# Attention with negated scores: the position bias and the row extreme in one VectorE instruction

## The chip, the cores and the metric

The kernel runs on one core of a Trainium2 chip. A core has a matrix engine (TensorE, PE in the profile, with its weight loads as PEld), VectorE (DVE), ScalarE (ACT), GpSimd (POOL) and SyncE (SP), which issues the transfers (DMA). The metric is device microseconds of one execution, as the median of several runs.

## The reference

One layer of a hybrid decoder: 2048 tokens of width 1024 are normalized, projected into three branches (attention, a short gated convolution, RWKV-7 time mixing), gated, projected back, added to the input and normalized again. The change is in the attention: four heads, each with two softmax maps of 64-wide queries and keys, whose difference is applied to V. A bias that depends on the distance of query and key is added to the scores, and keys after the query are masked.

```python
logits = jnp.einsum('bqhmd,bkhmd->bhmqk', qb, kf) + bias[None, :, None]
logits = jnp.where(dist >= 0, logits, NEG_INF)
p = jax.nn.softmax(logits, axis=-1)
a = p[:, :, 0] - lam * p[:, :, 1]
return jnp.einsum('bhqk,bkhd->bqhd', a, vf)
```

## The kernel before

Products are made in float32 split into a high and a low part (three products for each full one). The tokens come in two halves of 1024. The stages follow each other: the input projection of what RWKV needs, RWKV of the first half, attention of the first half (541 to 865 us in the profile), RWKV of the second half, attention of the second half (1217 to 1805 us), the rest of the output projection. While a stage runs, products of the input projection (`inproj`, L343) and later of the output projection (`out_tile`, L1194) are put between its own on TensorE, as filler. TensorE's order is written out by hand (the generators yield how much filler they want after each step; `run` and `pull` deal it out). The order on the other engines and on the DMA queue is chosen by a scheduler that simulates the program.

In `attention`, `scores` goes through row tiles of 128 queries of one head. The keys up to the row tile's own are cut into groups of at most 512 columns, and for each group and each of the two maps there is one score block: two products into a PSUM tile `S` (L937, L938), the bias added in place where the block meets it (L942), the negated row maximum into one column of `nm` (L943), and the exponential on ScalarE with `nm` as its bias, which also sums the row into `l` (L946). There are 96 blocks in the first half and 224 in the second.

The bias differs from a constant only for the last 128 distances. The constant falls out of the softmax, so a table `bt` of 128 x 384 for each head, made in `att_setup`, holds the rest and the mask. For row tile i it reaches from column (i - 1) x 128 to the tile's end: 256 columns, or the part of them that lies in the block.

`combine` brings the groups of a row tile to one maximum (L957 to L965) and mixes the two maps (L986). `values` transposes the mixed probabilities on TensorE (L1021) into `aT`, splits them into a high part `aTh` on ScalarE (L1027) and a low part `aTl` on VectorE (L1028), and multiplies both by V (L1012 to L1014). `load_k`, `load_q` and `load_v` fetch keys, queries and values through the DMA queue and split them on GpSimd. The queries get their factor of 0.125 when they leave the input projection (`att_steps`, `in_copy`, L368).

Of the kernel before, what the change touches and what calls it, by code (L numbers as in the profile page):

```python
# [13 lines left out]
AF = mybir.ActivationFunctionType  # L14
ALU = mybir.AluOpType
# [15 lines left out]
GW = 32 // NG  # L31
# [114 lines left out]
def trunk(ctx, tc, a, o, phases="RTO"):  # L146
# [65 lines left out]
    # row blocks of the gated mix, transposed: heads by 256 tokens, conv and rwkv by 512  # L212
# [12 lines left out]
    # ------------------------------------------------------------------ normalized input  # L225
    def stats(c):
        """1/rms of the tokens of a chunk of the second half, one column per 128 tokens."""
# [38 lines left out]
    def stats0(c, xs, pool, raw):  # L266
        """1/rms of the tokens, broadcast; with raw, the products with the unscaled input come first."""
# [40 lines left out]
    # ------------------------------------------------------------------ input projection  # L308
# [97 lines left out]
    def both(*steps):  # L406
        """The products of the steps, for the first chunk of all of them before the second."""
        for c in range(2):
            for f, args in steps:
                yield from f(*args, (c,))  # L410
            yield ("chunk", c)
# [9 lines left out]
    def att_steps(half, h):  # L421
        return [(in_copy, (half, T_K + h, f"k{h}", 1.0)), (in_v, (half, h)),
                (in_copy, (half, T_Q + h, f"q{h}", 0.125)), (in_silu, (half, T_ZA + h, f"za{h}"))]
# [30 lines left out]
    # ------------------------------------------------------------------ rwkv  # L454
    def rwkv(half, pool):
# [176 lines left out]
        def inverse(s):  # L632
            U, Z = s["U"], s["Z"]
            # inverses of the 32x32 diagonal blocks by forward substitution, GW columns of one block per partition;
            # the odd rows are first freed of the even rows before them, so that two rows go at a time
# [24 lines left out]
        def late(s):  # L660
# [30 lines left out]
            # [W | U0]  # L691
# [15 lines left out]
            # transition matrices and the read-out of the incoming state  # L707
# [38 lines left out]
            # group norm, bonus, gate  # L746
# [29 lines left out]
        def chain(n):  # L776
            """The way of a unit up to the inverse; the scores may not start before the unit two back has been read."""
# [36 lines left out]
    # ------------------------------------------------------------------ attention  # L814
    def att_setup(pool):
# [15 lines left out]
        for h in range(4):  # L831
# [3 lines left out]
            nc.gpsimd.memset(bz[:, 256:], NEG)  # L835
            cpy(bz[:, 0:256], bp[:, 0:256])
# [7 lines left out]
    def attention(half, nlam, bt, pool, after=None):  # L844
        """One softmax row tile (128 queries) after the other; the matrix products with V of the pairs of tiles
        that are finished lie between the score blocks of the next ones."""
# [532 lines left out]
```

## Time and profile before

| | |
|---|---|
| median of 3 runs | 1854.19 us (1853.9 to 1865.09) |
| span of the profiled execution | 1855.8 us |
| TensorE busy | 1723.0 us, 93% |
| VectorE busy | 1228.7 us, 66% |
| ScalarE busy | 737.5 us, 40% |
| GpSimd busy | 817.9 us, 44% |

Busy times are those of the engines' own instructions in one execution. A stage is read by its window: how long each engine was busy between two times, and at which share of full speed TensorE's clock was granted. A wait names the engine, tile and line that waited, what released it, the total, how often, and the longest. The chain of work that ended last is followed back from the last instruction, at each step to what released it.

### The profile page before, as it was taken

Reading aid. Unit: us, or ns where it says so; the run is one execution under the profiler, and the core shown is the slowest. Engines: PE = TensorE matmul, PEld = TensorE weight load, DVE = VectorE, ACT = ScalarE, POOL = GpSimd, SP = SyncE. Lnnn points to the kernel's source line nnn. Section 1 sums busy time; section 2 is a strip of 40 time slices with the busy share of each in tenths; the row PEclk is TensorE's granted clock in tenths of the full one; section 3 lists DMA queues with packets and bytes.
Section 4 is the critical chain, followed back from the end, with each engine's and each line's share of the span. In section 5 each row is a group of like instructions: output and inputs, shape, how many; then the busy total and the mean of one; then the engine's idle time right before and its main releaser. Section 6 shows DMA issues by size and latency. Waiting matters only on the chain.

```text
span 1855.8 us, 27286 instructions
## 1 busy us (share of the span) xinstructions
PE 1723.0 (93%) x9416; PEld 1288.3 (69%) x9416; DVE 1228.7 (66%) x2653; ACT 737.5 (40%) x1797; POOL 817.9 (44%) x786
## 2 busy tenths in 40 slices
PE   5899799999999889999799999999999989999998
PEld 4687576777776666777666767766666666767686
DVE  7534866656527888756766576357788888777742
ACT  5331111221126555532122221145565656666642
POOL 6443332333286776334222233473485473453233
PEclk8899898998999999999799998999999989999999
DMA  5342121222156442124222222351142243232223
GB/s 181 114 146 93 47 63 59 86 76 67 61 181 196 148 140 82 64 68 148 63 82 68 86 76 62 100 154 60 63 147 64 74 150 101 71 95 70 81 78 116
DMA packets 136586, 180.13 MB, mean 97 GB/s; under 512 B 34912, under 2 KB 83072, under 8 KB 136448
## 3 DMA queue, kind: packets, MB, share of 16 engines
q1 hardware_dynamic: 136448, 178.39, 30.8%
q8 instruction: 74, 1.21, 0.3%
q14 instruction: 64, 0.52, 0.1%
HBM read 132.18 MB, written 46.14 MB: 96 GB/s over the span
## 4 chain that ended last, share of the span: by engine, by line
PE 62%; DVE 25%; DMA 4%; issue 3%; SPq 2%; ACT 2%; POOL 1%; DVEq 0%; POOLq 0%; ACTq 0%
PE pj L343 27%; PE ops L1194 9%; PE S L938 6%; DVE tmpx L646 5%; PE aT L1021 3%; PE S L937 3%; DVE Xs L649 3%; PE G L572 2%; PE av L1012 2%; DVE P L986 2%; SPq L594 2%; PE av L1014 2%; PE av L1013 2%; DVE x L242 1%; DVE nm L943 1%
## 5 line engine op out<-in xcount | busy, mean ns | idle before, releaser
L343 PE MATMUL pj<-hh,wh 128*128 128x512 f32 x1008 | 424.4, 421 | 4.2 <-DVE raw L394 3.4
L343 PE MATMUL pj<-hl,wh 128*128 128x512 f32 x1008 | 423.8, 420 | 0.0
L343 PE MATMUL pj<-hh,wl 128*128 128x512 f32 x1008 | 423.2, 420 | 0.0
L946 ACT ACTIVATE P<-S,nm 128x512 f32<-128x512 f32 (+3 forms) x320 | 199.3, 623 | 162.9 <-DVE nm L943 143.6
L943 DVE TENSOR_REDUCE nm<-S 128x1 f32<-128x512 f32 (+3 forms) x320 | 192.5, 606 | 77.4 <-PE S L938 74.1
L329 POOL TENSOR_TENSOR wl<-wr,wh 128x1024 fp32r<-128x1024 f32 x85 | 209.6, 2465 | 46.8 <-ACT wh L324 41.2
L343 PEld LDWEIGHTS pj<-hh,wh 128*128 128x128 f32 x1008 | 195.9, 194 | 49.1 <-issue 7.6
L343 PEld LDWEIGHTS pj<-hl,wh 128*128 128x128 f32 x1008 | 195.7, 194 | 45.2 <-issue 9.7
L343 PEld LDWEIGHTS pj<-hh,wl 128*128 128x128 f32 x1008 | 195.4, 194 | 45.0 <-issue 7.9
L938 PE MATMUL S<-K,QL 64*128 64x512 f32 (+2 forms) x320 | 150.1, 469 | 0.0
L326 POOL TENSOR_SCALAR wh<-wr 128x1024 fp32r<-128x1024 f32 x70 | 76.5, 1093 | 162.5 <-PE pj L343 152.6
L986 DVE SCALAR_TENSOR_TENSOR P<-P,sc 128x512 f32<-128x512 f32 (+3 forms) x160 | 141.5, 910 | 4.5 <-ACT P L970 2.9
L646 DVE TENSOR_TENSOR tmpx<-U,Xs 128x16 f32<-128x16 f32 (+15 forms) x256 | 128.6, 502 | 6.6 <-POOL U L640 1.2
L938 PEld LDWEIGHTS S<-K,QL 64*128 64x128 f32 x320 | 58.8, 184 | 101.6 <-issue 99.4
L937 PE MATMUL S<-K,QH 128*128 128x512 f32 (+2 forms) x320 | 120.8, 378 | 8.0 <-ACT P L946 8.0
L1028 DVE TENSOR_TENSOR aTl<-aT,aTh 128x512 fp32r<-128x512 f32 x144 | 98.4, 686 | 35.2 <-ACT aTh L1027 34.4
L1027 ACT CAST aTh<-aT 128x512 fp32r<-128x512 f32 x144 | 83.7, 585 | 87.9 <-PE aT L1021 87.1
L942 DVE TENSOR_TENSOR S<-S,bt 128x256 f32<-128x256 f32 (+1 forms) x152 | 57.4, 379 | 90.6 <-PE S L938 86.6
L1021 PE MATMUL aT<-con,P 128*128 128x128 f32 x576 | 93.9, 289 | 22.4 <-DVE aTl L1028 17.4
L1194 PE MATMUL ops<-woh,wl 128*128 128x512 f32 x256 | 103.9, 406 | 0.0
L1194 PE MATMUL ops<-woh,wh 128*128 128x512 f32 x256 | 103.5, 404 | 0.0
L1194 PE MATMUL ops<-wol,wh 128*128 128x512 f32 x256 | 103.5, 404 | 0.0
(336 smaller groups left out, 3354.2 us busy)
## 6 DMA issues: line engine op xcount, KB each, us to landing
wr<-in_wt_dram SPq DMA_DIRECT2D x85, 512.0 KB, 3.7
rawk<-pk SPq DMA_DIRECT2D x96, 128.0 KB, 2.8
U<-ud SPq DMA_DIRECT2D x128, 64.0 KB, 2.2
rawq<-pq SPq DMA_DIRECT2D x128, 64.0 KB, 2.3
wr<-mx SPq DMA_DIRECT2D x128, 64.0 KB, 1.9
oxt<-in_x_dram SPq DMA_DIRECT2D x32, 256.0 KB, 3.2
out_dram<-oxt SPq DMA_DIRECT2D x32, 256.0 KB, 2.1
prw<-s SPq DMA_DIRECT2D x28, 256.0 KB, 2.1
```

The lines of the kernel that those rows point to most:

```text
L329: nc.gpsimd.tensor_tensor(wl[:, ks], wr[:, ks], wh[:, ks].bitcast(F32), ALU.subtract)
L343: mm(ps, lhs[:, k], rhs[c][k], start=(n == 0), stop=(n == 3 * NK - 1))
L646: tt(tmp[:, :, :, 0:m], U[:, 0:m, i:i + 2].rearrange("p j r -> p r j").unsqueeze(2).broadcast_to([P, 2, GW, m]), Xs[:, 0:m].rearrange("p j ...
L937: mm(s[:, 0:sw], QH[:, m, off:off + P], K[:, m, 0:sw], start=True, stop=False)
L938: mm(s[:, 0:sw], QL[ms, off:off + P], K[ms, m, 0:sw], start=False, stop=True)
L943: nc.vector.tensor_reduce(nm[:, m, g:g + 1], s[:, 0:gw], AX.X, ALU.max, negate=True)
L946: act(p[:, 0:gw], s[:, 0:gw], AF.Exp, bias=nm[:, m, g:g + 1], accum_out=l[:, m, g:g + 1])
L986: stt(p1, p1, sc[:, 1, g:g + 1], p0, ALU.mult, ALU.add)
L1021: nc.tensor.transpose(t[:, d * 256 + qi * P:d * 256 + qi * P + P], x["A"][g][:, ko:ko + P], ident)
L1027: cpy(th, t)
L1028: tt(tl, t, th.bitcast(F32), ALU.subtract)
L1194: mm(ps, l[:, k], Ws[n][r][k], start=(c == 0), stop=(c == 3 * NK - 1))
```

## The change

The queries' factor and the table get the other sign, so that the scores in PSUM are negated, and the smallest score of a row is what `nm` needs. In a block that meets the bias, the columns before the bias are reduced to their minimum first (where there are any), and then one instruction adds the table to the remaining columns, writes them back, and folds their minimum with the first one (or with a large number). The exponential multiplies by -1. In a block without bias only the kind of extreme changes (a minimum, not a negated maximum). The rest of the diff removes comments.

```diff
     def att_steps(half, h):
         return [(in_copy, (half, T_K + h, f"k{h}", 1.0)), (in_v, (half, h)),
-                (in_copy, (half, T_Q + h, f"q{h}", 0.125)), (in_silu, (half, T_ZA + h, f"za{h}"))]
+                (in_copy, (half, T_Q + h, f"q{h}", -0.125)), (in_silu, (half, T_ZA + h, f"za{h}"))]
...
             bz = pool.tile([P, 512], F32, name="bz", bufs=2)
-            nc.gpsimd.memset(bz[:, 256:], NEG)
-            cpy(bz[:, 0:256], bp[:, 0:256])
+            nc.gpsimd.memset(bz[:, 256:], -NEG)
+            act(bz[:, 0:256], bp[:, 0:256], AF.Copy, scale=-1.0)
...
                     lo, hi = max(b0, g0), g0 + gw
+                    low = nm[:, m, g:g + 1]
+                    free = min(lo, hi) - g0
+                    if free > 0:
+                        nc.vector.tensor_reduce(low, s[:, 0:free], AX.X, ALU.min)
                     if hi > lo:
                         bo = lo - (i - 1) * P
-                        tt(s[:, lo - g0:gw], s[:, lo - g0:gw], bt[h][:, bo:bo + hi - lo], ALU.add)
-                    nc.vector.tensor_reduce(nm[:, m, g:g + 1], s[:, 0:gw], AX.X, ALU.max, negate=True)
+                        nc.vector.tensor_tensor_reduce(s[:, free:gw], s[:, free:gw], bt[h][:, bo:bo + hi - lo], 1.0,
+                                                       low if free > 0 else -NEG, ALU.add, ALU.min, low)
                     p = pool.tile([P, CK], F32, name="P", bufs=pb)
                     live[0] += 1
-                    act(p[:, 0:gw], s[:, 0:gw], AF.Exp, bias=nm[:, m, g:g + 1], accum_out=l[:, m, g:g + 1])
+                    act(p[:, 0:gw], s[:, 0:gw], AF.Exp, bias=low, scale=-1.0, accum_out=l[:, m, g:g + 1])
```

Lines after this place are five higher in the changed kernel (L986 is L991, L1028 is L1033, L1063 is L1068), those just before it one or none.

The first place is on VectorE, at the start of the first attention stage. A row is an instruction: its line, its kind, what it writes and reads, and the size. Before, a block is an add (L942) and a reduction (L943):

```order
L942 TENSOR_TENSOR S<-S,bt_701 128x128
L943 TENSOR_REDUCE nm<-S 128x1
L967 RECIPROCAL sc<-l 128x2
L1028 TENSOR_TENSOR aTl<-aT,aTh 128x512
L974 TENSOR_SCALAR sc<-sc,nlam 128x1
L942 TENSOR_TENSOR S<-S,bt_701 128x128
L986 SCALAR_TENSOR_TENSOR P<-P,sc 128x384
L943 TENSOR_REDUCE nm<-S 128x1
```

The same place in the changed kernel:

```order
L944 TENSOR_REDUCE nm<-S 128x1
L947 ISA S,nm<-S,bt_701,nm 128x128
L947 ISA nm 128x1
L972 RECIPROCAL sc<-l 128x2
L1033 TENSOR_TENSOR aTl<-aT,aTh 128x512
L979 TENSOR_SCALAR sc<-sc,nlam 128x1
L944 TENSOR_REDUCE nm<-S 128x1
L991 SCALAR_TENSOR_TENSOR P<-P,sc 128x384
L947 ISA S,nm<-S,bt_701,nm 128x128
L947 ISA nm 128x1
```

A block with free columns is now a reduction of these (L944), the fused instruction (L947, here "ISA", which reads `nm` too) and a second one of one column that writes the result to `nm`. A block without free columns is the last two alone. In all, 152 adds and 320 reductions before are 256 reductions, 152 fused instructions and 152 of one column after.

The second place is on VectorE, later in the first attention stage. The numbers are those of the buffers; `S_6121` before is `S_6105` after, the block of the same products, and `aTl_6134` is `aTl_6118`. Before:

```order
L1061 SCALAR_TENSOR_TENSOR ob_5947<-ob_5947,der_76,obc_6104 128x256
L986 SCALAR_TENSOR_TENSOR P_5735<-P_5735,sc_6098,P_5721 128x128
L986 SCALAR_TENSOR_TENSOR P_5703<-P_5703,sc_6098,P_5678 128x512
L942 TENSOR_TENSOR S_6121<-S_6121,bt1_710 128x256
L1028 TENSOR_TENSOR aTl_6134<-aT_6128,aTh_6133 128x512
L943 TENSOR_REDUCE nm_6062<-S_6121 128x1
```

After:

```order
L1066 SCALAR_TENSOR_TENSOR ob_5931<-ob_5931,der_76,obc_6088 128x256
L944 TENSOR_REDUCE nm_6046<-S_6105 128x1
L991 SCALAR_TENSOR_TENSOR P_5691<-P_5691,sc_6082,P_5666 128x512
L947 ISA S_6105,nm_6046<-S_6105,bt1_710,nm_6046 128x256
L947 ISA nm_6046 128x1
L1033 TENSOR_TENSOR aTl_6118<-aT_6112,aTh_6117 128x512
L991 SCALAR_TENSOR_TENSOR P_5721<-P_5721,sc_6082,P_5708 128x128
```

`aTl` stood ahead of the block's reduction and now stands behind the whole block. Of the 144 instructions of this kind, 20 are moved behind one or more further blocks in this way, and one ahead of one; of the 160 of L986, 24 are behind one more and 16 behind one fewer.

The third place is on the DMA queue, in the first attention stage: loads of keys (`rawk`), queries (`rawq`), gates (`zs`) and weights (`wr`), and stores of what the input projection made (L354) and of the attention's result (`mx`). Before:

```order
L1063 DMA mx_1_93<-ob 128x256
L998 DMA zs<-pza_0_4566 128x256
L856 DMA rawk<-pk_0_5373 64x512 x4
L354 DMA pv_0_5601<-t_5599 128x512
L884 DMA rawq<-pq_1_4444 64x256 x4
L320 DMA wr<-in_wt_dram 128x1024
```

After:

```order
L1003 DMA zs<-pza_0_4566 128x256
L320 DMA wr<-in_wt_dram 128x1024
L856 DMA rawk<-pk_0_5365 64x512 x3
L884 DMA rawq<-pq_1_4444 64x256 x2
L354 DMA pv_0_5589<-t_5587 128x512
L884 DMA rawq<-pq_1_4444 64x256 x2
L856 DMA rawk<-pk_0_5365 64x512
L320 DMA wr<-in_wt_dram 128x1024
```

The fourth load of the keys' tile is now behind loads of queries and a store.

## Rows read from the trace of the kernel before

**Rows 1.** The page: span, and busy time of two engines.
```profile
span 1855.8 us, 27286 instructions
PE 1723.0 (93%) x9416; PEld 1288.3 (69%) x9416; DVE 1228.7 (66%) x2653; ACT 737.5 (40%) x1797; POOL 817.9 (44%) x786
```

**Rows 2.** Windows: both attention stages, then a stretch of the first.
```profile
core 0: us, PE busy (x) PEld busy (x) DVE busy (x) ACT busy (x) POOL busy (x), PEclk, DMA share, GB/s
541.00:865.00 324.00, 304.30 (x1466) 223.97 (x1465) 233.26 (x508) 167.14 (x448) 191.85 (x196) 0.98 0.39 123
1217.00:1805.00 588.00, 567.96 (x2669) 402.07 (x2668) 454.73 (x856) 351.74 (x849) 285.26 (x253) 0.98 0.29 91
...
590.00:700.00 110.00, 96.28 (x455) 69.07 (x454) 90.35 (x189) 60.21 (x157) 84.00 (x81) 0.95 0.50 155
```

**Rows 3.** TensorE's waits, 541 to 865 us: total us, times, longest.
```profile
PE aT L1021 <- DVE aTl L1028: 10.0, 6, 3.4
PE av L1014 <- DVE aTl L1028: 4.9, 2, 4.2
```

**Rows 4.** TensorE's waits, 1217 to 1805 us.
```profile
PE aT L1021 <- DVE aTl L1028: 7.4, 6, 4.4
PE S L937 <- ACT P L946: 7.0, 6, 2.9
...
PE aT L1021 <- DVE P L986: 2.1, 1, 2.1
```

**Rows 5.** The chain by line: 541 to 865, 1217 to 1805, 590 to 700 us.
```profile
by line: PE pj L343 41.0%; PE S L938 8.5%; PE aT L1021 4.3%; PE S L937 4.2%; DVE P L986 4.1%; DVE xk L242 3.3%; PE av L1012 3.1%; DMA xk<-in_xT_dram 3.0%; PE av L1014 3.0%; PE av L1013 2.4%; DVE nm L943 2.4%; DVE aTl L1028 2.3%; issue 2.1%;
...
by line: PE ops L1194 21.0%; PE pj L343 15.9%; PE S L938 12.8%; PE aT L1021 8.5%; PE S L937 7.0%; PE av L1012 4.9%; PE av L1014 3.9%; PE av L1013 3.9%; DVE P L986 3.8%; issue 2.2%; DVE nm L943 1.9%; DVE wol L1153 1.5%; POOL K L864 1.4%; ACT
...
by line: PE pj L343 18.8%; DVE xk L242 9.8%; DMA xk<-in_xT_dram 8.9%; DVE P L986 8.8%; PE S L938 6.5%; DVE nm L943 5.4%; issue 4.3%; DVE aTl L1028 3.9%; DVE S L942 3.8%; DVE hl L246 3.4%; PE aT L1021 3.4%; PE S L937 3.2%; PE av L1014 2.7%; 
```

**Rows 6.** VectorE's groups by shape: count, busy us, mean ns, idle before.
```profile
L943 DVE TENSOR_REDUCE nm<-S 128x1 f32<-128x512 f32 x224 | 152.4, 685 | 75.8 <-PE S L938 74.1
...
L942 DVE TENSOR_TENSOR S<-S,bt 128x256 f32<-128x256 f32 x96 | 41.1, 428 | 47.6 <-PE S L938 44.7 <-ACT P L946 2.6
...
L943 DVE TENSOR_REDUCE nm<-S 128x1 f32<-128x384 f32 x32 | 17.6, 551 | 0.4
...
L942 DVE TENSOR_TENSOR S<-S,bt 128x128 f32<-128x128 f32 x56 | 16.3, 294 | 43.0 <-PE S L938 41.8 <-ACT P L946 0.8 <-ACT e L959 0.3
...
L943 DVE TENSOR_REDUCE nm<-S 128x1 f32<-128x256 f32 x32 | 13.5, 420 | 0.6
...
L943 DVE TENSOR_REDUCE nm<-S 128x1 f32<-128x128 f32 x32 | 9.2, 288 | 0.6
```

**Rows 7.** Single lines: count, duration in ns (least, median, most), forms.
```profile
L504 DVE TENSOR_TENSOR_SCAN e__1195<-conr,e x1: 692/692/692, 157.0 to 157.0; 128x256 f32<-128x256 f32 x1
...
L1206 DVE TENSOR_TENSOR oss<-oss x16: 146/928/1890, 1530.1 to 1850.2; 128x1 f32<-128x1 f32 x16
...
L957 DVE TENSOR_REDUCE mn<-nm x48: 142/150/162, 569.4 to 1767.1; 128x2 f32<-128x4 f32 x16, 128x2 f32<-128x6 f32 x16, 128x2 f32<-128x8 f32 x16
```

**Rows 8.** Small instructions: groups of VectorE and ScalarE, two of the timeline.
```profile
L964 DVE RECIPROCAL lr<-lr 128x2 f32<-128x2 f32 x48 | 7.9, 165 | 1.5
...
588.24 0.15 DVE L1053 TENSOR_SCALAR ors<-ovp 128x2 f32<-128x2 f32 x1
588.31 0.15 DVE L235 TENSOR_TENSOR ss<-ss 128x4 f32<-128x4 f32 x1
...
L946 ACT ACTIVATION_READ_ACCUMULATOR P<-S,nm 128x1 f32 x320 | 62.7, 196 | 0.0
```

**Rows 9.** Windows, 590 to 700 us: L943 alone, then L942 alone.
```profile
590.00:700.00 110.00, 19.74 (x38) 0.95 0.50 155
...
590.00:700.00 110.00, 11.17 (x30) 0.95 0.50 155
```

**Rows 10.** Waits of the whole span, GpSimd for a load of K.
```profile
POOL K L861 <- DMA rawk<-pk: 18.4, 10, 5.7
```

## The prediction

> **What bounds the kernel now.** I read the stage windows first [rows 1, 2]. TensorE is busy for 1723.0 of 1855.8 us, VectorE for 1228.7. The changed code runs in the two attention stages only: 541 to 865 us and 1217 to 1805 us. There TensorE is busy 304.3 of 324 us (94%) and 568.0 of 588 us (97%), VectorE 233.3 (72%) and 454.7 us (77%). So TensorE bounds both stages, and all its idle time in them is 19.7 + 20.0 us. A faster VectorE can only give back what part of these 39.7 us it causes.
>
> Next come TensorE's waits in the same windows [rows 3, 4]. What VectorE causes directly: 10.0 + 4.9 us in the first stage and 7.4 + 2.1 us in the second, 24.4 us together. Another 7.0 us in the second stage is a wait for ScalarE's exponential, whose input VectorE prepares. 31.4 us is thus a ceiling for any gain by way of VectorE. Most of these waits are for aTl (the low part of the transposed probabilities), which this change does not touch: it only stands behind other work in VectorE's queue.
>
> One stretch is denser than the rest. From 590 to 700 us VectorE is busy 90.35 of 110 us, TensorE only 96.28, and the granted clock is 0.95 [rows 2]. In the chain of work that ended last, the reduction (nm L943) has 2.4% of the first stage, 1.9% of the second, but 5.4% of that stretch, where the bias add (S L942) has another 3.8% [rows 5].
>
> **What the change does to VectorE's busy time.** A score block is 128 queries by up to 512 keys. Of 320 blocks, 152 meet the bias (96 adds of 256 columns, 56 of 128 [rows 6]); 168 are as before. From the loops, with the widths as (block = free + biased):
>
> - 128 = 0+128, 32 blocks: 288 + 294 ns become 294 ns and a read of the accumulator;
> - 256 = 0+256, 32 blocks: 420 + 428 become 428 and a read;
> - 384 = 128+256, 32 blocks: 551 + 428 become 288 + 428 and a read;
> - 512 = 256+256, 32 blocks: 685 + 428 become 420 + 428 and a read;
> - 512 = 384+128, 24 blocks: 685 + 294 become 551 + 294 and a read.
>
> The reductions are rows of their widths [rows 6]. The two new costs have no row.
>
> The fused main instruction passes over as many columns as the add it replaces, from the same PSUM tile and the same table. I take the add's 428 and 294 ns, which is also the lower end, since none of its columns goes away. The upper end is the one row of an instruction that carries a value from column to column, the scan: 692 ns at 256 columns [rows 7], 264 more than the add; at 128 columns half of that, 132 more.
>
> The read of the accumulator (a second instruction, 128x1) I take as the reciprocal of two columns, 165 ns. Lower end 70 ns: two small independent rows start at 588.24 and 588.31. Upper end: ScalarE's own accumulator read, 196 ns [rows 8].
>
> With the taken values the five kinds of block save 123, 255, 98, 100 and -31 ns: 3.9 + 8.2 + 3.1 + 3.2 - 0.7 = **17.7 us of VectorE's busy time**, 1.4% of its total. With a read of 70 ns it is 17.7 + 152 x 0.095 = 32.1 us; with the scan's rate and a read of 196 ns it is 17.7 - 96 x 0.264 - 56 x 0.132 - 152 x 0.031 = -19.7 us, a loss.
>
> [...]
>
> A rule speaks against the change: the instruction count grows from 304 to 392 (88 blocks need three instructions instead of two). The reduction's rows put a price on this: from 128 to 512 columns it grows by 397 ns, 1.03 ns a column, so about 156 ns are fixed [rows 6]. 88 more instructions are 13.7 us; the 31,744 biased columns that are no longer passed over twice are 32.8 us. [...] By count alone VectorE would get 13.7 us more work; the rows show that the columns weigh more.
>
> **What of it reaches the end.** In the dense stretch the two lines have 9.2% of the chain, 10.1 us, of their 19.74 + 11.17 = 30.9 busy us [rows 5, 9]: a share of 0.33. Elsewhere the reduction has 7.8 + 11.2 - 5.9 = 13.1 us on the chain of 192.7 - 19.7 = 173.0 busy us [rows 5, 6, 9]: 0.076. 30 of the 152 changed blocks lie in the dense stretch [rows 9]. So 3.5 us saved there give 1.2 us, 14.2 us elsewhere 1.1 us: **-2.3 us**. The rest is hidden behind TensorE, which is 94 to 97% busy.
>
> Against this stands the order. TensorE's order does not change by a row. On the other queues the scheduler placed work anew, and 20 times aTl now stands behind the later instructions of one more block (second place of the change's rows). Counting each move as a full reduction of 0.685 us, it is 13.7 us if TensorE waited for all of them. It waited for 6 + 2 + 6 = 14 of 144 [rows 3, 4], so I take a tenth: **+1.3 us**.
>
> The other edits cost nothing that the rows can show: the sign of q's factor, of the exponential's scale and of the table are arguments of instructions that stay. The four copies of the table become ScalarE activations with a scale before the attention begins, under the projection's products. Were they on the path, four of at most 0.7 us are 3 us.
>
> The sum against the profile's own span: 1855.8 - 2.3 + 1.3 = 1854.8 us. The median of the runs is 1854.19, 1.6 us below the span, so the forecast is **1853.2 us**: no change that a measurement can tell (about 1%, 18.5 us, is what one of this kernel can).
>
> **The rivals.**
>
> - *The main instruction runs at the scan's rate* (the change doesn't do what it says). It then adds 96 x 0.264 + 56 x 0.132 = 32.7 us, net +15.0 us of VectorE: dense 3.0 x 0.33, elsewhere 12.0 x 0.076, +1.9 us, with the order's 1.3: 1857 us. For it: it must keep a running extreme. Against: the plain reduction keeps one too, and its 256 columns take 420 ns, less than the add. [...]
> - *The new order costs more.* On the DMA queue a load of K that stood as four in a row is now split by loads of Q and a store of V (third place). GpSimd has waited up to 5.7 us for such a load [rows 10]. Half of the 20 moved aTl on the path are +6.9, less 2.3: 1859 us. For it: every queue but TensorE's was placed anew. Against: of those 14 waits for aTl none is longer than 4.4 us, and a reduction is 0.7 us.
> - *The accumulator read stalls* (the other side: slower). Small VectorE rows can be long: the one-column add L1206 has a median of 928 ns and reaches 1890 [rows 7]. If the read took 0.93 us like it, VectorE would get 152 x 0.765 - 17.7 = +98.6 us. 19.5 us of these fall in the dense stretch, where VectorE has just 19.65 us idle, so there they pass whole; elsewhere 79.1 x 0.076 = 6.0: +25.5, with the order 1881 us. It decides (1%) where 30 dense blocks and 122 x 0.076 = 9.3 others, 39.3 in effect, lose 18.5 us: 0.47 us each beyond the 0.12 saved, a read of 0.75 us. Against: the reduction L957, which reads and writes the same small tiles, is never longer than 162 ns [rows 7].
> - *The waits go away* (faster). Some 60% of the ceiling of 31.4 us would have to vanish for 1%; with two thirds it is 1833 us. Nothing speaks for so much but the clock of 0.95 in the dense stretch, which could rise with fewer pauses.
>
> **How the numbers follow.** Forecast 0.48, new order 0.25, scan's rate 0.12, stalled read 0.08, waits gone 0.07. The middle three quarters lie near 1853 to 1859. Low end: a read of 70 ns (32.1 us saved: 6.3 x 0.33 + 25.8 x 0.076 = 4.0), no moved aTl waited for, and a fifth of the 31.4 us lost to a luckier order: 1844. High end: scan's rate (+1.9) and half of the moved aTl (+6.9): 1863, with the slack of a microsecond 1864. About 2 in 10 is left outside. Faster by over 1% 0.05 (most of the last rival), slower by over 1% 0.08 (the stalled read), within 1% 0.87.
>
> **What would show it.** In the profile after: the main instruction at 256 columns near 428 ns (692 would be the scan's rate), the read near or under 165 ns, VectorE's busy time near 1211 us, TensorE's busy time unchanged, its waits for aTl near the 22.3 us of before, and the dense stretch still the place with the most idle time. I am wrong if the read is over 0.75 us, if TensorE's idle time in the attention stages falls below 20 us in all, or if a new line (a load of K or Q) leads its waits.

## The result: slower by 0.6%, outside the range

The changed kernel takes 1866.9 us (median of 20 runs, 1857.6 to 1875.6); the kernel before, beside it, 1854.6 us. The ratio is 1.0064, with a 95% interval of 1.0047 to 1.0082. It is within 1%, as most of the chance said, but it is a loss of 12 us where 1 us of gain was forecast, and the range ended at 1864 us.

The first lines of the profile after (span, instructions, busy time of the engines), against [rows 1]:

```profile
span 1857.8 us, 27402 instructions
...
PE 1718.1 (92%) x9416; PEld 1283.2 (69%) x9416; DVE 1209.4 (65%) x2741; ACT 735.3 (40%) x1797; POOL 813.7 (44%) x786
```

This execution, with 1859.6 us of its own, is one of the quickest of the 20. Its span is just 2.0 us longer than that of [rows 1], so the loss has to be looked for by stage. Between the two attention stages it is 9.5 us shorter than before (420.4 against 429.9 us), but that stretch takes 432.6 us in a second profile of the same changed kernel (run *again*, below), so this is no steady effect of the change. The two stages that hold the changed code did get longer. A stage is measured here from the weight load of its first score product to that of its last one. Each line gives these two starting times, the first two lines for the kernel before and the last two for the one after:

```profile
L937 PEld LDWEIGHTS S<-K,QH x96: 186/188/330, 541.1 to 789.2; 128*128 128x128 f32 x96
L937 PEld LDWEIGHTS S<-K,QH x224: 186/188/337, 1219.1 to 1764.5; 128*128 128x128 f32 x112
L938 PEld LDWEIGHTS S<-K,QH x96: 187/188/330, 543.5 to 796.7; 128*128 128x128 f32 x96
L938 PEld LDWEIGHTS S<-K,QH x224: 186/188/337, 1217.1 to 1766.8; 128*128 128x128 f32 x112
```

The first stage takes 248.1 us before and 253.2 after, the second 545.4 and 549.7. That is +9.4 us.

VectorE did what the change says. Its busy time fell by 19.3 us, from 1228.7 to 1209.4. The new instructions (groups by shape: count, busy us, mean ns, idle time before):

```profile
L947 DVE CUSTOM_DVE_ANT_0 S<-S,bt,nm 128x256 f32<-128x256 f32 x64 | 31.3, 489 | 2.4
L947 DVE DVE_READ_ACCUMULATOR2_ANT nm<- 128x1 f32 x152 | 21.4, 141 | 0.0
L947 DVE CUSTOM_DVE_ANT_0 S<-S,bt 128x256 f32<-128x256 f32 x32 | 13.7, 429 | 23.4 <-PE S L939 23.3
...
L947 DVE CUSTOM_DVE_ANT_0 S<-S,bt 128x128 f32<-128x128 f32 x32 | 9.6, 299 | 38.8 <-PE S L939 38.8
...
L947 DVE CUSTOM_DVE_ANT_0 S<-S,bt,nm 128x128 f32<-128x128 f32 x24 | 8.4, 353 | 0.6
```

A form without a first value runs at the add's rate of [rows 6] (429 against 428 ns, 299 against 294). A form that starts from `nm` takes 54 to 60 ns more. The read of the accumulator takes 141 ns, but it starts before its main instruction has ended (597.75 + 0.43 us against 598.10 in one block); the median read ends 58 ns after the main instruction.

So less work made the stages longer. TensorE's waits in the first stage (541 to 865 us) and the second (1217 to 1805 us): total us, times, longest. They answer to [rows 3, 4]:

```profile
PE aT L1026 <- DVE aTl L1033: 11.8, 7, 3.1
PE av L1019 <- DVE aTl L1033: 4.9, 4, 2.6
PE aT L1026 <- DVE ors L1058: 2.7, 2, 1.7
PE av L1017 <- ACT aTh L1032: 2.1, 1, 2.1
...
PE S L938 <- ACT P L951: 9.6, 7, 2.7
PE aT L1026 <- DVE aTl L1033: 7.8, 10, 2.3
```

The waits for aTl rose only from 22.3 to 24.5 us. Others are new or longer: `ors` (2.7 against 1.1 us), a ScalarE copy (aTh) that TensorE did not wait for before, and the exponential (9.6 against 7.0 us).

The waits and the clock together account for the longer stages. All waits of TensorE over 0.15 us grew from 16.0 to 20.5 us in the first stage and from 19.8 to 21.6 in the second; the time at half the clock (a granted share of 0.50) grew by 3.4 us in each (13.7 to 17.1, 20.5 to 23.9). If half of that time counts as lost, which is an estimate, this is +9.7 us for the +9.4 measured. By the same count, what is left of a stage after its waits and its lost clock is 224 to 227 us and 514 to 518 us in all 17 profiles of this study.

### The profile page after: what moved, and what is told of

It reads as the page before. It is cut to its first block, busy times and chain, and to the rows that moved or that the text cites. A ratio compares the mean times of both kernels' runs of the same rounds, so it can differ in the third digit from the quotient of the medians.

```text
span 1857.8 us, 27402 instructions
## 1 busy us (share of the span) xinstructions
PE 1718.1 (92%) x9416; PEld 1283.2 (69%) x9416; DVE 1209.4 (65%) x2741; ACT 735.3 (40%) x1797; POOL 813.7 (44%) x786
## 4 chain that ended last, share of the span: by engine, by line
PE 61%; DVE 25%; DMA 4%; issue 3%; ACT 2%; SPq 2%; POOL 1%; DVEq 0%; POOLq 0%; ACTq 0%
PE pj L343 27%; PE ops L1199 9%; PE S L939 5%; DVE tmpx L646 5%; PE aT L1026 3%; PE S L938 3%; DVE Xs L649 3%; DVE P L991 2%; PE av L1017 2%; PE G L572 2%; PE av L1019 2%; PE av L1018 2%; SPq L594 2%; DVE nm L944 1%; DVE x L242 1%
## 5 line engine op out<-in xcount | busy, mean ns | idle before, releaser
L944 DVE TENSOR_REDUCE nm<-S 128x1 f32<-128x512 f32 (+3 forms) x256 | 150.0, 589 | 117.4 <-PE S L939 116.5
L991 DVE SCALAR_TENSOR_TENSOR P<-P,sc 128x512 f32<-128x512 f32 (+3 forms) x160 | 144.4, 930 | 6.3 <-ACT P L975 4.0
L1033 DVE TENSOR_TENSOR aTl<-aT,aTh 128x512 fp32r<-128x512 f32 x144 | 98.2, 686 | 44.2 <-ACT aTh L1032 44.2
L1026 PEld LDWEIGHTS aT<-con,P 128*128 128x128 f32 x576 | 64.6, 144 | 53.5 <-DVE aTl L1033 18.2
```

Source lines behind the costliest of these rows:

```text
L944: nc.vector.tensor_reduce(low, s[:, 0:free], AX.X, ALU.min)
L991: stt(p1, p1, sc[:, 1, g:g + 1], p0, ALU.mult, ALU.add)
L1026: nc.tensor.transpose(t[:, d * 256 + qi * P:d * 256 + qi * P + P], x["A"][g][:, ko:ko + P], ident)
L1033: tt(tl, t, th.bitcast(F32), ALU.subtract)
```

## The experiments

Two theories stood against each other. **Order**: the scheduler, given other durations and other instructions, placed the work of VectorE, ScalarE, GpSimd and the DMA queues anew, and the new order makes TensorE wait. **Instructions**: the 88 blocks with three instructions instead of two, the dearer form and the read delay the exponentials.

The table gives each run beside the kernel before on the same chip, then both attention stages of its profiled execution (first to last weight load of a score product) and their sum. One profile's stage can differ by some 3 us from the next one's of the same kernel, and the sum by 6 (*after* and *again*), so the sum is read together with the ratio.

| run | ratio (95%) | stages, us | sum |
|---|---|---|---|
| before (the profile of the rows above) | 1 | 248.1, 545.4 | 793.5 |
| after (the changed kernel) | 1.0064 (1.0047 to 1.0082) | 253.2, 549.7 | 802.9 |
| again | 1.0060 (1.0033 to 1.0087) | 256.6, 552.6 | 809.2 |
| new_ops_old_order | 0.9968 (0.9941 to 0.9994) | 245.5, 545.2 | 790.7 |
| ops_in_old_order_2 | 0.9983 (0.9956 to 1.0010) | 247.2, 545.2 | 792.4 |
| old_ops_new_order | 1.0100 (1.0071 to 1.0128) | 257.0, 555.3 | 812.3 |
| negated_only | 1.0005 (0.9977 to 1.0033) | 248.9, 545.7 | 794.6 |
| new_order_att0 | 1.0011 (0.9989 to 1.0033) | 254.5, 543.7 | 798.2 |
| places_undone | 0.9989 (0.9963 to 1.0016) | 249.0, 545.1 | 794.1 |
| old_pool_order | 1.0073 (1.0037 to 1.0109) | 258.0, 554.8 | 812.8 |
| new_pool_order | 0.9999 (0.9978 to 1.0021) | 249.7, 543.6 | 793.3 |
| one_atl_forward | 1.0048 (1.0012 to 1.0084) | 252.9, 550.8 | 803.7 |
| one_wl_later | 1.0037 (1.0007 to 1.0067) | 248.1, 552.8 | 800.9 |
| two_wl_later | 1.0023 (0.9999 to 1.0048) | 253.1, 549.2 | 802.3 |
| fuse_free0_only | 0.9999 (0.9979 to 1.0019) | 252.9, 540.4 | 793.3 |
| fuse_free_only | 1.0041 (1.0017 to 1.0066) | 259.0, 549.0 | 808.0 |
| mixed_order | 0.9976 (0.9951 to 1.0001) | 250.7, 543.2 | 793.9 |

### Operations and order, apart

The mark first: the changed kernel once more.

> The changed kernel once more, as the mark for the three others on the same chip. Every theory expects the ratio already measured, 1.004 to 1.009 of the time before (about 1862 to 1871 us), and a second profiled execution in which VectorE is busy 1209 us again, with the two attention stages longer than before by about 5 and 4 us.

It came out at 1.0060, with VectorE busy for 1209.6 us. The stages, 256.6 and 552.6 us, are each 3 us longer than in the first profile; the profiled execution, 1875.2 us, is one of the longest of its kernel. Next, the two parts of the change that a diff does not separate. A table holds an order for each engine, and edges that fix only the order of issue, without a wait, put the instructions into it before they are scheduled; what it takes from the other kernel is the order alone:

```diff
     with tile.TileContext(nc, schedule_with_timeline_sim=True) as tc:
         trunk(tc, aps, {"out": out[0]})
+        replay(tc, nc)
...
+    for eng, text in ORDER.items():
+        pos = np.cumsum(np.frombuffer(zlib.decompress(base64.b85decode(text)), np.int16).astype(int))
...
+        for x, y in zip(pos, pos[1:]):
+            tc.add_manual_dep(mine[y], mine[x].name, mybir.DependencyInfo(
+                mybir.DependencyClass.NoSync, mybir.DependencyReason.DATA), reason="order")
```

> All the instructions of the change (reduce of the free part, one add-and-minimum, its read, the negated signs), but on VectorE, ScalarE, GpSimd and the DMA queues in the order in which the kernel before has them: the fused instruction stands where the row maximum stood, the reduce of the free part where the add stood (for 12 blocks, the first of their row tile, directly ahead of the fused one). If the new order costs the time (theory 'order'), this has VectorE's saving of 19 us and none of the cost: 0.997 to 1.001 of before, 1849 to 1856 us. If the new instructions cost it (theory 'instructions': the fused one 60 ns dearer with a pointer, 141 ns of read, later start of the exponential), it stays at 1.004 to 1.009, 1862 to 1871 us.

> The kernel before, its arithmetic unchanged, with the four engines' instructions in the order that the changed kernel has (an add that has no partner there stands directly ahead of its row maximum). Theory 'order': 1.005 to 1.010 of before, since the new order comes without VectorE's saving (1864 to 1873 us). Theory 'instructions': 0.998 to 1.002, 1851 to 1858 us.

Measured: 0.9968 for the new operations in the old order, 1.0100 for the old operations in the new order. Their product is 1.0068, and both together were measured at 1.0064 and 1.0060. TensorE's waits in the first stage, new operations in the old order:

```profile
PE aT L1026 <- DVE aTl L1033: 9.0, 6, 2.3
PE av L1019 <- DVE aTl L1033: 5.0, 3, 3.6
PE aT L1026 <- DVE ors L1058: 1.1, 2, 0.7
```

And old operations in the new order:

```profile
PE aT L1021 <- DVE aTl L1028: 13.2, 8, 3.4
PE av L1014 <- DVE aTl L1028: 5.9, 4, 2.6
PE aT L1021 <- DVE ors L1053: 3.0, 2, 1.6
PE av L1012 <- ACT aTh L1027: 2.8, 1, 2.8
```

The second list is that of the changed kernel, including the wait for aTh, though not one of its instructions is the change's. The order is the cause of the loss. The operations alone measured 0.3% faster here and 0.2% in a second run (*ops_in_old_order_2*, below), whose interval holds 1: a small gain, or none.

The third part is the signs of the change's diff (query factor, table, scale of the exponential) with the add and the reduction still apart. It keeps every engine's order as it was before. Against the kernel before, in the score block:

```diff
                         tt(s[:, lo - g0:gw], s[:, lo - g0:gw], bt[h][:, bo:bo + hi - lo], ALU.add)
-                    nc.vector.tensor_reduce(nm[:, m, g:g + 1], s[:, 0:gw], AX.X, ALU.max, negate=True)
+                    nc.vector.tensor_reduce(low, s[:, 0:gw], AX.X, ALU.min)
```

> The negated scores alone: query scale -0.125, bias table negated, row minimum in place of the negated maximum, exponential with scale -1; the add and the reduction remain two instructions, and every engine has the order of before. Both theories expect no change, 0.998 to 1.002 of before (1851 to 1858 us); a third one, that the signs cost something (an exponential with a scale, the query eviction, the bias table), expects 1.004 or more.

1.0005: the signs cost nothing that shows.

### Which part of the order

TensorE's order is the same in all these kernels, so the idle time ahead of one and the same TensorE instruction can be compared from trace to trace. Four instructions have a long wait in all three traces with the new order (after, again, old operations in the new order) that is short or absent in the three with the old one: the aT product near 602 us (3.1 us against 0.5), the av product near 649 (2.1 to 2.8 against 0), the aT product near 683 (3.1 to 3.4 against 1.0 to 1.2) and a score product near 1643 (2.7 to 2.9 against 0). The reverse exists too: near 697 us the old order waits 2.3 to 3.4 us where the new one waits 0.0 to 0.2 (and 1.6 to 1.7 a few products on, where the old one waits for nothing), and near 1507 the old one waits 4.4 to 4.5 where the new one waits 2.1 to 2.7. The place near 649 is mostly such an exchange within itself: two products on, the old order waits 3.6 to 4.2 us for aTl (the longest of av in [rows 3]) and the new one 2.6 to 2.9, so that both waits together are 4.7 to 5.3 us against 3.6 to 4.2.

The two orders differ only within short groups of rows, which can be exchanged one by one. Four runs did that (the rows of one stage, of four neighbourhoods, or of GpSimd). The edit is the table of the order; in words:

```diff
-    order = new                                                     # the changed kernel
+    order = new in the first stage, old in the second               # new_order_att0
+    order = new, but old at 592-606, 643-652, 676-686, 1624-1648 us # places_undone
+    order = new, but old for GpSimd                                 # old_pool_order
+    order = old, but new for GpSimd                                 # new_pool_order
```

> The changed kernel's instructions, with its new order in the first attention stage (and the few moved rows of the RWKV stage behind it) and the order of before in the second. If the whole cost of the order lies in a few places of the first stage (the aT wait of 3.1 us that all three traces with the new order show near 602 us, and two more near 649 and 683), the stage from its first to its last score product takes 253 to 257 us as in the changed kernel (246 in the old order) and the second 545 to 546 as in the old order: 1.001 to 1.005 of before. If the cost is spread over both in proportion to their length, one third of it is left: 0.998 to 1.001.

> The changed kernel in its new order, but with the order of before in four short neighbourhoods: those around the waits of TensorE that all three traces with the new order have and none with the old one (near 602, 649, 683 and 1643 us). Theory 'few places': these four waits (3.1, 2.1, 3.1 and 2.7 us) and the two drops of the granted clock that follow the first and the last are gone, and the time is within 4 us of the changed operations in the old order, 0.996 to 1.001 of before. Theory 'spread': the waits show up elsewhere, and the time stays at 1.003 to 1.008.

> The changed kernel, with GpSimd's instructions alone in the order of before; VectorE, ScalarE and the DMA queues keep the new one. Theory 'overlap': what costs is which VectorE instructions fall under GpSimd's two-operand instructions (a 2-element VectorE scalar multiply took 2.29 us and ended when GpSimd's 2.35 us subtraction of the weights ended), so putting GpSimd's back takes away at least the waits near 602 and 1643 us: 0.997 to 1.003. Theory 'VectorE's own order': GpSimd's order matters little and it stays at 1.003 to 1.008.

> The reverse: the changed kernel's instructions in the order of before on VectorE, ScalarE and the DMA queues, and GpSimd's alone in the new order. Theory 'overlap': a good part of the cost comes back, 1.001 to 1.006 of before, with VectorE instructions that hold SBUF operands alone stretched where GpSimd's long ones now lie. Theory 'VectorE's own order': as the changed operations in the old order, 0.994 to 0.999.

With the new order in the first stage alone, the stages come out as "few places" has them (254.5 us, and 543.7 like the old order's 545); the ratio, 1.0011 against 0.9968 and 0.9983 with none of the new order, lies at the border of both theories. With the four neighbourhoods undone it is 0.9989: of the 0.8% between 1.006 and 0.998, 0.7% go, as "few places" expected. Its waits from 590 to 700 us:

```profile
PE av L1019 <- DVE aTl L1033: 4.1, 1, 4.1
PE aT L1026 <- DVE aTl L1033: 2.5, 2, 2.0
```

The waits near 602 (0.55 us) and 1643 (none) went as expected, with the low clock behind them. The other two did not quite: near 649 the old order's own wait of 4.1 us came back, and near 683 2.0 us are left. So most of the gain has to come from the first and the last place. GpSimd's order alone is neither the cure (1.0073, 5 runs) nor the cause (0.9999), so "overlap", put as a matter of GpSimd's order, missed both its numbers. With GpSimd's old order the wait near 602 us does fall from 3.1 to 1.8 us and that near 1643 from 2.7 to 1.9, yet others come.

### What happens at such a place

Near 602 us the changed kernel's VectorE, GpSimd and TensorE (timeline: start, us, line, tiles, and idle time before):

```profile
599.18 0.53 DVE L970 TENSOR_TENSOR sc<-e,lr 128x4 f32<-128x4 f32 x1
599.74 2.29 DVE L979 TENSOR_SCALAR sc<-sc,nlam 128x2 f32<-128x2 f32 x1
601.95 0.68 DVE L1033 TENSOR_TENSOR aTl<-aT,aTh 128x512 fp32r<-128x512 f32 x1
...
599.65 2.35 POOL L329 TENSOR_TENSOR wl<-wr,wh 128x1024 fp32r<-128x1024 f32 x1
...
602.68 1.12 PE L1026 MATMUL aT<-con,P 128*128 128x128 f32 x4 [3.09 <-DVE aTl L1033]
```

A scaling of two elements takes 2.29 us, from 599.74 to just after 602.00, when GpSimd's subtraction of 2.35 us ends. Behind it stands aTl, ready since about 601, and TensorE waits 3.09 us. In the kernel before, VectorE at this place has aTl first, then the same scaling (0.91 us):

```profile
597.04 0.67 DVE L1028 TENSOR_TENSOR aTl<-aT,aTh 128x512 fp32r<-128x512 f32 x1
...
597.82 0.91 DVE L974 TENSOR_SCALAR sc<-sc,nlam 128x2 f32<-128x2 f32 x1
```

The wait costs more than itself. Windows after: from 601.4 to 608.2 us the granted clock is 0.50, after TensorE had stood still since 599.6. Near 1642 us, the place of the fourth wait, it is the same. The first two lines are after, the last two before:

```profile
601.40:608.20 6.80, 5.52 (x18) 4.47 (x19) 3.49 (x5) 1.52 (x4) 2.81 (x4) 0.50 0.38 121
1642.40:1649.30 6.90, 5.24 (x17) 4.09 (x17) 5.17 (x16) 4.79 (x14) 3.24 (x4) 0.51 0.30 95
...
596.40:603.30 6.90, 6.19 (x35) 4.73 (x35) 6.80 (x14) 3.42 (x9) 6.58 (x7) 1.00 0.57 173
1642.40:1649.30 6.90, 6.40 (x37) 4.88 (x36) 6.21 (x18) 6.21 (x17) 6.06 (x8) 1.00 0.45 142
```

The kernel before gets 35 and 37 products done at these places, at a clock of 1.00, and the changed one 18 and 17.

The fourth place has the same anatomy. After, VectorE has two combining products ahead of the score blocks, and GpSimd a rounding remainder and a weight subtraction beside them:

```profile
1636.24 5.31 DVE L991 SCALAR_TENSOR_TENSOR P<-P,sc 128x512 f32<-128x512 f32 x2
...
1641.55 0.35 DVE L947 CUSTOM_DVE_ANT_0 S<-S,bt,nm 128x128 f32<-128x128 f32 x1
...
1637.07 1.62 POOL L864 TENSOR_TENSOR K<-rawk,K 64x512 fp32r<-64x512 f32 x1
1638.64 2.36 POOL L1180 TENSOR_TENSOR wl<-wr,wh 128x1024 fp32r<-128x1024 f32 x1
...
1642.90 0.58 PE L938 MATMUL S<-K,QH 128*128 128x256 f32 x1 [2.65 <-ACT P L951]
```

Two products take 5.31 us. The second of them takes 4.09, to 1641.55, where the median is 0.74; GpSimd has finished both of its instructions at 1641.00. The next score block's add and minimum starts at 1641.55, its exponential after that, and TensorE waits 2.65 us for the buffer.

Over the whole span, lines of VectorE fall into two kinds (least, median and most ns). These have SBUF operands alone:

```profile
L979 DVE TENSOR_SCALAR sc<-sc,nlam x64: 198/228/3502, 548.2 to 1770.8; 128x1 f32<-128x1 f32 x16, 128x2 f32<-128x2 f32 x16, 128x3 f32<-128x3 f32 x16, 128x4 f32<-128x4 f32 x16
...
L991 DVE SCALAR_TENSOR_TENSOR P<-P,sc x160: 336/744/4093, 549.8 to 1774.6; 128x512 f32<-128x512 f32 x112, 128x128 f32<-128x128 f32 x16, 128x256 f32<-128x256 f32 x16, 128x384 f32<-128x384 f32 x16
```

And this one reads PSUM and one SBUF operand:

```profile
L1033 DVE TENSOR_TENSOR aTl<-aT,aTh x144: 664/691/694, 560.5 to 1795.4; 128x512 fp32r<-128x512 f32 x144
```

The first kind is long only where GpSimd works beside it: the 55 combining products of 512 columns that no GpSimd instruction overlaps take 733 to 753 ns, the other 57 take 736 to 4093; the 24 scalings beside none take 205 to 231 ns, the other 40 take 198 to 3502. aTl keeps to 664 to 694 ns, though 25 of the 144 lie beside two-operand instructions of GpSimd for over 95% of their time. By what means GpSimd lengthens the first kind is not shown. The change's own fused instruction (PSUM and table) stays undisturbed: 429 ns at 256 columns where the add had 428, and 495 at most in any form.

Two runs tested this place by moving one row each:

```diff
 VectorE (one_atl_forward)
+aTl<-aT,aTh
 sc<-e,lr
 sc<-sc,nlam
-aTl<-aT,aTh
```

```diff
 GpSimd (one_wl_later)
-wl<-wr,wh
 P<-P,sc
 K<-rawk
+wl<-wr,wh
```

> The changed kernel with one VectorE instruction moved: the aTl of the place near 602 us stands two rows earlier, ahead of the product sc and of the scaling of sc by nlam (as in the order of before), all else as in the changed kernel. Theory 'order at the place': the aT product that waited 3.1 us for this aTl in three traces waits under 0.8, the granted clock does not drop near 601, and the first stage (253.5 to 256.9 us from first to last score product) is 3 to 6 us shorter. The time alone falls too little to be told from the changed kernel's: 1.002 to 1.006 of before. Rival: the lost time comes back at the next aTl, and the stage stays at 253 or more.

> The changed kernel with one GpSimd instruction moved: the 128x1024 subtraction wl near 600 us stands two rows later, behind the scaling of P and the rounding of K; VectorE's order is the changed kernel's. Theory 'overlap': the 2-element scaling of sc on VectorE, 2.29 us under wl in the changed kernel, takes less than 1.2 us, since what lies beside it now is shorter (0.58 and 1.04 us), the aTl behind it starts sooner, and the aT product's wait of 3.1 us shrinks by 1 us or more. Rival: the scaling is long for a reason of its own (its scalar comes from another engine, its two elements), and stays over 2 us. The time of the whole: 1.002 to 1.007 of before in both.

With aTl moved forward (timeline, then TensorE's waits from 590 to 610 us):

```profile
597.71 0.67 DVE L1033 TENSOR_TENSOR aTl<-aT,aTh 128x512 fp32r<-128x512 f32 x1
...
598.49 2.26 DVE L979 TENSOR_SCALAR sc<-sc,nlam 128x2 f32<-128x2 f32 x1
...
598.30 2.42 POOL L329 TENSOR_TENSOR wl<-wr,wh 128x1024 fp32r<-128x1024 f32 x1
```

```profile
PE av L1019 <- DVE aTl L1033: 2.3, 1, 2.3
PE aT L1026 <- DVE ob L1066: 0.6, 1, 0.6
PE aT L1026 <- DVE aTl L1033: 0.2, 1, 0.2
```

The wait of 3.1 us falls to 0.2 and the clock does not drop near 601, but the scaling still takes 2.26 us, and the next aTl pays: 2.3 us ahead of the av product, 0.5 before. The stage (252.9 us) is no shorter than that of the changed kernel, where 3 to 6 us were expected. The rival was right in this.

With GpSimd's subtraction moved instead (timeline, then waits):

```profile
596.12 0.23 DVE L979 TENSOR_SCALAR sc<-sc,nlam 128x2 f32<-128x2 f32 x1
596.25 0.69 DVE L1033 TENSOR_TENSOR aTl<-aT,aTh 128x512 fp32r<-128x512 f32 x1
...
596.19 0.61 POOL L977 TENSOR_SCALAR P<-P,sc 128x384 f32<-128x384 f32 x1
...
599.25 2.36 POOL L329 TENSOR_TENSOR wl<-wr,wh 128x1024 fp32r<-128x1024 f32 x1
```

```profile
PE aT L1026 <- DVE aTl L1033: 1.0, 1, 1.0
PE av L1019 <- DVE aTl L1033: 0.7, 1, 0.7
```

The scaling takes 0.23 us, the wait falls to 1.0, the clock stays at 1.00 from 596 to 606 us, and nothing comes back at the next aTl (0.7 against 0.5). So it is the overlap that made the scaling long, not its kind or its size. The time, 1.0037, cannot be told from the changed kernel's. A second such row, near 1639 us, was then moved too:

```diff
 GpSimd (two_wl_later, beside the row of one_wl_later)
-wl<-wr,wh
 oss<-oss,mexp
 P<-   (memset)
+wl<-wr,wh
```

> The changed kernel with two GpSimd rows moved, the subtraction wl near 600 us (two rows later, as before) and the one near 1639 us (behind the row-sum powers oss and a memset); VectorE, ScalarE and the DMA queues keep the changed kernel's order. Theory 'stretching': both waits of TensorE near 602 and 1643 us (3.1 and 2.7) fall under 1.2, the combining product of 4.08 us near 1637 is at most 2.9, and the stages shorten by 4 to 8 us together: 1.000 to 1.004 of before. Theory 'place on VectorE': the wait near 1643 stays over 2 us, and the time at 1.004 to 1.008.

The same combining products and the same score product (which stand near 1646 us in this profile):

```profile
1642.13 2.98 DVE L991 SCALAR_TENSOR_TENSOR P<-P,sc 128x512 f32<-128x512 f32 x2
...
1646.45 0.39 PE L938 MATMUL S<-K,QH 128*128 128x256 f32 x1 [0.33 <-ACT P L951]
```

The score product waits 0.3 us instead of 2.7, that near 602 1.0 instead of 3.1, the combining product of 4.09 us is gone (none from 1600 to 1700 us takes over 2), and the time is 1.0023, within what "stretching" expected. But the interval of this run and that of the changed kernel's 1.0064 just touch, the 4 to 8 us by which the stages should have shortened did not come in this profile (802.3 us against 802.9 and, in *again*, 809.2), and the clock still fell for 3.4 us after a wait of 1.5 us at the next aT product. So that these two rows make the two waits is shown, and how much of the time they bring back is not.

### Parts of the change, and a better order

```diff
-                    if hi > lo:
+                    if hi > lo and (free <= 0):
...
+                    else:
+                        if hi > lo:
+                            bo = lo - (i - 1) * P
+                            tt(s[:, lo - g0:gw], s[:, lo - g0:gw], bt[h][:, bo:bo + hi - lo], ALU.add)
+                        nc.vector.tensor_reduce(low, s[:, 0:gw], AX.X, ALU.min)
```

This is fuse_free0_only; fuse_free_only has `free > 0` in that condition.

> The changed kernel, with the one-instruction form only in the 64 blocks that lie under the bias as a whole (no part is free of it); the other 88 add and reduce the whole block as before, with the minimum. The order is the scheduler's own. It inherits the late aTl near 602 us, not the moved combining products near 1643. VectorE's saving by the traced durations: 32 x (0.29 - 0.14) + 32 x (0.42 - 0.14) = 13.8 us of 19.3. Theory 'order': 0.999 to 1.005 of before, with a wait near 3 us near 602 and none near 1643. Theory 'instructions' (the 88 three-instruction blocks are the dear ones): 0.995 to 0.998.

> The reverse: the one-instruction form only in the 88 blocks that have a part free of the bias (reduce of that part, then the fused instruction that starts from it), the other 64 as before. The order is the scheduler's own; it leaves the aTl near 602 us where it was, and moves others of the first stage and the second. VectorE's saving is the rest, 5 to 6 us. Theory 'order': no wait over 1 us near 602, but new ones elsewhere: 0.999 to 1.006 of before. Theory 'instructions': all of the cost, 1.005 to 1.009.

Each part gets an order of its own from the scheduler. The 64 blocks alone: 0.9999, with a wait of 1.1 us near 602 where 3 was expected and none near 1643. The 88 alone: 1.0041, with the wait near 602 gone, another of 2.4 us a few products earlier, and one of 2.6 near 1643. The first matches "order" by its time but not by its place near 602. The second matches it by its time and, but for the wait of 2.4 us just ahead of that place, by its places; its interval does not rule out "instructions". The first part loses nothing, and the second cannot be told from the whole: with an order that comes out anew each time, such runs do not divide the loss between the two forms.

Last, an order put together from both: the old one, with the new one at the two places where it waits less.

```diff
-    order = old
+    order = old, but new at 687-706 and 1486-1508 us
```

> The changed operations in the order of before, with the new order in two neighbourhoods where the traces show it better (the aT waits of 2.3 to 3.4 us near 697 and of 4.4 us near 1507 are 0 to 0.2 and 2.1 to 2.7 with it). If the waits of a place follow from its own order alone: 2 to 4 us less than the changed operations in the old order, 0.993 to 0.996 of before. If they hang on the rows far ahead: 0.996 to 1.000.

> The changed operations in the order of before once more, as the mark for the mixed order on the same chip: 0.994 to 0.999 of before.

The waits there changed as meant (0.0 us near 697, though 1.7 us a few products on; 2.7 near 1507 against 3.5), but 0.9976 and 0.9983 cannot be told apart, and the 2 to 4 us less that a wait with a cause of its own place would give do not show. The changed operations in the old order, or in this one, are the quickest kernels of the study, by 0.2 to 0.3%, with two of the three intervals reaching 1.

## Why the prediction was wrong, step by step

- **VectorE's saving: right in number, in part by luck.** 17.7 us were worked out, 19.3 measured. The main instruction without a first value is the add to 5 ns. Two terms were off and nearly cancel: the 88 that start from `nm` are 54 to 60 ns dearer (+5.3 us), the read is 141 instead of 165 ns (-3.6 us). So the durations of the blocks' lines fall by 15.8 us (reductions 192.7 to 149.9, fused 63.0 for the adds' 57.4, reads 21.4). But durations that overlap are not busy time: the read adds 58 ns to its main instruction, not 141. Without the blocks' lines VectorE is busy for 1015.9 us before and 1024.2 after, so the blocks save 27.6 us, nearer to the prediction's low end (a read of 70 ns, 32.1 us), and the other lines, which the prediction left as they were, take 8.3 more.
- **The count of instructions did not decide.** 88 more instructions, and VectorE's busy time still fell by 19.3 us: the columns weighed more, as the rows said.
- **What reaches the end of it: not contradicted.** -2.3 us were forecast; in the old order the operations gave ratios of 0.9968 and 0.9983, some -6 and -3 us, with intervals that hold -2.3 but reach from -11 to +2.
- **The signs cost nothing: right**, to 0.3% (1.0005, 0.9977 to 1.0033).
- **The order, +1.3 us: wrong, by more than ten times.** This is the step that failed. The new order costs 1.0% with the old operations (18 us) and 0.9% with the new (1.0064 over 0.9976, the mean of the two runs in the old order: 16 us). "Counting each move as a full reduction of 0.685 us" priced an aTl that moves behind other rows by a kind of row whose length is constant for its width (685 ns on average at 512 columns, 670 to 694). The place near 602 us shows what an aTl is moved behind: the product sc and a scaling of two elements, which take 0.37 us at their least in the changed kernel's trace (157 + 215 ns) and 2.8 here, beside GpSimd's subtraction. This aTl moved behind no score block, so it is not even among the 20 that were counted. And the tenth, taken from the 14 of 144 aTl that TensorE waited for, spread over all aTl what a few places hold. The count of moved aTl missed the place near 1643 us altogether, where it is combining products that moved ahead of score blocks, and that near 649, where ScalarE's copy to aTh was put behind an exponential and waits with it (a place that costs some 1 us on balance).
- **The rival "The new order costs more"** named the right cause and was less than half as large as it should be: +6.9 for +16 to +18, since it too used 0.685 us a move, and left out the lower clock after a long wait. So did the ceiling of 31.4 us: before, 34 us of the two stages ran at half the clock. Its sentence against, "none is longer than 4.4 us", was no comfort. Its chance was 0.25 against the forecast's 0.48, although the edit let four queues be placed anew beside an engine that is idle for just 40 of 912 us, and none of the prediction's own signs of being wrong covered it: the read took 0.14 us, TensorE's idle time did not fall below 20 us, and no load led its waits.
- **The rows stood there.** [rows 7] has the one-column add L1206 at 146, 928 and 1890 ns, and the prediction used it for the read of the accumulator alone, which reads no tile and was never longer than 145 ns. As a price for *rows that other rows are queued behind*, it would have widened the range.
- **The other rivals fall**: the scan's rate (429 and 489 ns, not 692), the stalled read (132 to 145 ns), the waits that vanish.
- **The dense stretch** of [rows 2] was rightly named: three of the four places lie from 590 to 700 us, and the granted clock of this stretch fell:

```profile
590.00:700.00 110.00, 96.71 (x440) 69.53 (x440) 84.69 (x202) 57.33 (x155) 82.16 (x82) 0.92 0.47 141
```

VectorE is busy there for 5.7 us less than before, and TensorE gets 440 products done in place of 455, at a clock of 0.92 instead of 0.95.

What stays open: whether all of the order's cost is such overlap. The waits of two of the four places, near 602 and 1643 us, are shown to come from it. At 649 and 683 us the rows look alike (VectorE rows of 1.5 to 1.8 us beside GpSimd's, score work behind them), but no run took that away there alone.

## What to carry to other kernels

Where a scheduler places the instructions, an edit is two changes: its operations, and a new order for everything near it. Run them apart (new operations in the old order, and the reverse) before judging either; here they were -0.2 to -0.3% and +0.9 to +1.0%. And when an instruction moves in a queue, price the high end of it by the longest that the rows ahead of it ever take, not by their mean: least, median and most of a line tell whether it has a length of its own at all.

## What the runs showed of the hardware

- A VectorE instruction of two elements took 0.23 us, or 2.29 us beside a GpSimd subtraction of 2.35 us, in the same program but for one GpSimd row's place.
- The fused add-and-minimum runs at the plain add's rate from PSUM (429 against 428 ns at 256 columns, 299 against 294 at 128); a first value read from a tile adds 54 to 60 ns (489 against 429 at 256 columns, 353 against 299 at 128). The read of its result is a second instruction of 132 to 145 ns, of which 58 ns (median) come after the end of the first.
- Near 602 and 1643 us, waits of TensorE of 2.7 to 3.1 us were followed by 3.4 to 6.8 us at half the clock in all three traces with the new order (after, again, old_ops_new_order). If half of that time counts as lost, an estimate, each cost 0.6 to 1.3 times its own length again.
